# Three 256-column matmuls in place of a 512- and a 256-column one, and products summed to SBUF before the norm is applied

## The chip, the cores and the metric

One NeuronCore of a Trainium2 chip runs the program. The metric is the device time of one execution in microseconds (us); of several executions the median stands. The profile comes from one more execution. Engines: TensorE (PE, with its weight loads PEld), VectorE (DVE), ScalarE (ACT), GpSimd (POOL), and SyncE (SP), whose queue issues the weight transfers.

## What is computed

Two transformer blocks, one after the other, on 256 tokens of width 1024, in float32. The reference in short:

```python
x = x + 0.5 * swiglu(rms_norm(x, ffn1_norm), ...)             # first feed-forward, inner width 2816
z = rms_norm(x, mix_norm) @ w_in + b_in                       # first mixer: window attention and mLSTM
x = x + merged(z) @ w_out
x = rms_norm(x + 0.5 * swiglu(rms_norm(x, ffn2_norm), ...), final_norm)   # second feed-forward
h = x
proj = rms_norm_2(h, norm_mix_2) @ w_in_2                     # second mixer: gated linear attention and MLA
h = h + concat(o_gla, o_mla) @ w_out_2
h = h + cross_attention(rms_norm_2(h, norm_xa_2), mem) @ xa_w_o_2
g = conv3(rms_norm_2(h, norm_ffn_2) @ ffn_w_gate_2)           # third feed-forward, convolved along the tokens
h = h + (silu(g) * (rms_norm_2(h, norm_ffn_2) @ ffn_w_up_2)) @ ffn_w_down_2
```

## The kernel before

The activation `x` stays in SBUF, transposed: eight tiles of 128 features by 256 tokens, held in four pairs `x2[0..3]`. Every weight is read from HBM once, in chunks of up to 1 MB, by `wraw` (L327, three buffers `wr`). `halves` (L337) splits each chunk into a rounded part `wh`, by a ScalarE copy (L345), and the rest `wl`, by a VectorE subtraction (L346); both have six buffers. Activations are split in the same way by `split` (L458); a split tile holds the high part in `[:, 0]` and the low part in `[:, 1]`.

A product is the sum of high·high, high·low and low·high. `mm3` (L365) does this for one 128x128 block of a weight with two matmuls: `wh` against both parts side by side (512 columns: the left 256 get high·high, the right 256 high·low), then `wl` against the high part, added into the right 256. So one block of a product fills a PSUM bank of 512 columns in two parts, and `joined` (L520) adds them: ScalarE copies the right part to SBUF (L526), VectorE adds the left part (L527), and, if a norm `r` is given, VectorE multiplies it in (L529). `lin_t` (L377) is a product of 256 output features (2 x 8 blocks) into one PSUM tile of two banks; `lin_first` (L404) is the same with its last two blocks held back, into two tiles of another pool; `lin_n` (L386) computes with tokens in the partitions, three matmuls a block.

PSUM has eight banks. The pool `mm` has two tiles of two banks (`pm`, L228), the pool `at` four tiles of one bank (`pa`, L235). A tile is given again when all its readers have finished.

The norm factor `r` of a stage is ready late: squares, a sum on TensorE, `rsqrt` on GpSimd (L427, eleven small instructions) and `by_token` (L507), which spreads it over the partitions with TensorE. Products are therefore computed from the unnormalised `x`, and the norm is multiplied in when a product is joined.

The stages, in `program` (L1490): `ffn`, `mix` (L610), `ffn`, `mix2` (L966, with `mix2_heads` L998 and `xa` L1374), `ffn` with the convolution. In `ffn` (L533), `products(pr)` computes a gate and an up product and keeps both PSUM tiles in `pairs`; the loop at L565 joins, multiplies and splits them into `ahl`. Then four output tiles `dp`, each 2 x 22 blocks (L591 to L601), are joined, scaled and added to `x2[dp]`, and `x_done` (L448) splits the two new tiles of `x` for the next stage; in the last stage a DMA each writes them out (L607). In `mix`, three query products are started early (L619 to L621); `biased` (L624) joins a product into a tile `z` (two buffers) with the norm, and ScalarE adds the bias into the tiles `aq` (L631). In `mix2`, after the heads, the output projection (`wo2`, L982 to L995) adds two parts to each `x[d]` (L993, L994); in `xa` four query products (L1385) take tiles of `at`, and the output projection (`xo`, L1464 to L1484) again adds two parts to each `x` (L1476, L1483).

The order of the instructions on each engine is not the order of the program text: a planner simulates the program at compile time and lists the instructions by readiness, with the program order as the priority. Each engine then runs its list strictly in order.

Of the kernel before, what the change touches and what calls it, by code (L numbers as in the profile page):

```python
# [15 lines left out]
ALU = mybir.AluOpType  # L16
# [171 lines left out]
class Builder:  # L188
# [4 lines left out]

    def __init__(self, ctx, tc, I, out):
# [8 lines left out]
        self.uid = 0  # L203
        self.fine = 1
# [23 lines left out]
    def pm(self):  # L228

        return self.mm.tile([P, 2, 512], F32, tag="mm", name=self.n("mm"))  # L230

    def banks(self):
        return [t[:, j, :] for t in (self.pm(), self.pm()) for j in range(2)]
# [143 lines left out]
    def lin_t(self, key, xs, kt=KD, early=False):  # L377

        hv = self.wcols(key, 2, kt, early=early)
        ps = self.pm()  # L380
# [5 lines left out]
    def lin_n(self, key, n, xs, kt=KD, pool=None):  # L386

        ps = [pool() for _ in range(TB)] if pool else self.pm()
        ps = ps if pool else [ps[:, b, :] for b in range(TB)]
# [143 lines left out]
    def ffn(self, f, half, nxt=None, conv=False, last=False, first=False, mem=False):  # L533
# [3 lines left out]
        with self.phase("ffn") as fp:  # L537
# [5 lines left out]
            def products(pr):  # L543
# [4 lines left out]
                pairs[pr] = pg, self.lin_t(f"{f}u{pr}", xs, early=first and pr == 0)  # L548
# [16 lines left out]
            for pr in range(KF // 2):  # L565
                if pr > 1:
                    products(pr)
                pg, pu = pairs.pop(pr)
                s = ft([P, 512], "s", 2)
                if conv:  # L570
                    g = ft([P, 2, T + 2], "g", 2)
                    nc.vector.memset(g[:, :, 0:2], 0.0)
                    self.joined(pg, g[:, :, 2:], r)
                    for j in range(2):
                        w = [self.col("cw3", 22 * t + 2 * pr + j) for t in range(3)]
                        sj = s[:, j * T:j * T + T]
                        nc.scalar.activation(sj, g[:, j, 2:], AF.Identity, scale=w[2], bias=self.col("cb3", 2 * pr + j))
                        nc.vector.scalar_tensor_tensor(sj, g[:, j, 1:T + 1], w[1], sj, ALU.mult, ALU.add)
                        nc.vector.scalar_tensor_tensor(sj, g[:, j, 0:T], w[0], sj, ALU.mult, ALU.add)
# [6 lines left out]
                self.split(ahl[:, :, 2 * pr:2 * pr + 2, :].rearrange("p s j t -> p s (j t)"), a)  # L586
# [4 lines left out]
            for dp in range(KD // 2):  # L591
                ps = self.pm()
# [942 lines left out]
```

## Time and profile before

| | us |
|---|---|
| three runs | 1047.07, 1042.86, 1040.52 |
| their median | 1042.86 |
| the profiled execution | 1041.34 |
| its span, first to last instruction | 1039.6 |
| PE busy in the span | 998.3 |
| DVE busy | 753.4 |
| ACT busy | 598.8 |

The profiled execution took 1.7 us more than its span, and 1.5 us less than the median of the runs. A busy PE counts each matmul from its start to its end; matmuls overlap, so the pace of the array is read from the starts. PEclk is the granted clock of TensorE as a share of 2.4 GHz; its mean over the span is 0.988.

### The profile page before, as it was taken

What the parts mean: (1) busy time and instruction counts of PE and PEld (TensorE: products, weight loads), DVE (VectorE), ACT (ScalarE), POOL (GpSimd) and SP (SyncE); (2) the same over time, 40 slices, a digit from 0 to 9 for tenths busy, and PEclk for the clock granted to TensorE, in tenths of its full rate; (3) what the DMA queues carried; (4) which work ended last, traced back from release to release, by engine and by line L of the source; (5) the groups of instructions that cost most, each with busy time, mean ns of one, the idle gap of its engine ahead of it and who ended that gap; (6) DMA issues with size and microseconds to landing.
All of it is one profiled execution on the core that took longest, in us unless ns stands there. A gap on an engine that the chain in (4) does not pass through costs nothing.

```text
span 1039.6 us, 14827 instructions
## 1 busy us (share of the span) xinstructions
PE 998.3 (96%) x5562; PEld 848.6 (82%) x5562; DVE 753.4 (72%) x1309; ACT 598.8 (58%) x1041; POOL 66.1 (6%) x200
## 2 busy tenths in 40 slices
PE   6999999989999999999999999999899889999997
PEld 5888888879776778878888888987677768888886
DVE  7877666657977558787777856779848677988752
ACT  5755544448756456645655644669735456666541
POOL 4200000010000001000100200022000301000000
PEclk9999999999999999999999999999999989999999
DMA  6754555544444324544555555456006325555450
GB/s 240 252 202 173 182 180 192 193 152 173 134 170 142 122 81 168 197 162 170 203 195 202 200 178 202 138 212 223 22 1 243 122 81 198 172 197 192 161 195 20
DMA packets 28504, 172.72 MB, mean 166 GB/s; under 512 B 3712, under 2 KB 5008, under 8 KB 10128
## 3 DMA queue, kind: packets, MB, share of 16 engines
q1 hardware_dynamic: 26640, 169.88, 45.9%
q10 hardware_dynamic: 1728, 1.88, 0.7%
q8 instruction: 43, 0.70, 0.3%
q14 instruction: 29, 0.24, 0.1%
q0 software_dynamic: 64, 0.02, 0.0%
HBM read 170.72 MB, written 1.05 MB: 165 GB/s over the span
## 4 chain that ended last, share of the span: by engine, by line
PE 88%; DVE 4%; DMA 2%; ACT 2%; POOL 1%; issue 1%; ACTq 0%; DVEq 0%
PE mm L368 44%; PE mm L369 22%; PE mm L373 3%; PE mm L375 3%; PE mm L374 3%; DVE wl L346 2%; PE at L368 2%; DMA wr<-in_wts 1%; PE at L666 1%; PE at L702 1%; PE at L369 1%; ACT wh L345 1%; PE at L697 1%; DMA x<-in_xt 1%; PE at L807 0%
## 5 line engine op out<-in xcount | busy, mean ns | idle before, releaser
L346 DVE TENSOR_TENSOR wl<-wr,wh 128x1024 fp32r<-128x1024 f32 (+5 forms) x380 | 393.2, 1046 | 192.2 <-ACT wh L345 190.5
L345 ACT ACTIVATE wh<-wr 128x1024 fp32r<-128x1024 f32 (+5 forms) x380 | 340.5, 915 | 317.8 <-PE mm L368 222.6
L368 PE MATMUL mm<-xs,wh 128*128 128x512 f32 x1296 | 459.5, 399 | 9.2 <-DVE z L527 4.6
L369 PE MATMUL mm<-xs,wl 128*128 128x256 f32 x1296 | 364.2, 281 | 0.2 <-DVE wl L346 0.2
L368 PEld LDWEIGHTS mm<-xs,wh 128*128 128x128 f32 x1296 | 244.6, 189 | 67.7 <-issue 10.8
L369 PEld LDWEIGHTS mm<-xs,wl 128*128 128x128 f32 x1296 | 246.2, 190 | 0.9 <-DVE wl L346 0.6
L368 PE MATMUL mm<-ahl,wh 128*128 128x512 f32 x528 | 184.3, 395 | 0.0
L369 PE MATMUL mm<-ahl,wl 128*128 128x256 f32 x528 | 147.7, 280 | 0.0
L368 PEld LDWEIGHTS mm<-ahl,wh 128*128 128x128 f32 x528 | 99.0, 188 | 23.0
L369 PEld LDWEIGHTS mm<-ahl,wl 128*128 128x128 f32 x528 | 99.7, 189 | 0.0
L373 PE MATMUL mm<-wh,xs 128*128 128x512 f32 (+2 forms) x160 | 60.9, 381 | 2.0 <-ACT wh L345 2.0
L375 PE MATMUL mm<-wh,xs 128*128 128x512 f32 (+2 forms) x160 | 60.9, 381 | 0.0
L374 PE MATMUL mm<-wl,xs 128*128 128x512 f32 (+2 forms) x160 | 60.8, 380 | 0.0
L368 PE MATMUL mm<-b,wh 128*128 128x512 f32 x128 | 45.7, 397 | 0.0
L373 PEld LDWEIGHTS mm<-wh,xs 128*128 128x128 f32 x160 | 30.1, 188 | 7.8 <-ACT wh L345 2.3
L369 PE MATMUL mm<-b,wl 128*128 128x256 f32 x128 | 36.1, 282 | 0.0
L368 PE MATMUL at<-xs,wh 128*128 128x512 f32 x64 | 27.0, 462 | 8.4 <-DVE xs L467 8.4
L375 PEld LDWEIGHTS mm<-wh,xs 128*128 128x128 f32 x160 | 30.1, 188 | 5.8 <-issue 1.0
L374 PEld LDWEIGHTS mm<-wl,xs 128*128 128x128 f32 x160 | 30.1, 188 | 4.9
L368 PEld LDWEIGHTS mm<-b,wh 128*128 128x128 f32 x128 | 24.0, 188 | 6.0 <-issue 0.8
L585 DVE TENSOR_TENSOR a<-s,a 128x512 f32<-128x512 f32 x33 | 22.7, 692 | 2.8 <-ACT s L582 1.4
L368 PE MATMUL mm<-vs,wh 128*128 128x512 f32 x64 | 22.6, 395 | 1.9 <-DVE z L527 1.5
(503 smaller groups left out, 1242.3 us busy)
## 6 DMA issues: line engine op xcount, KB each, us to landing
wr<-in_wts SPq DMA_DIRECT2D x141, 1024.0 KB, 4.8
wr<-in_wts SPq DMA_DIRECT2D x12, 768.0 KB, 4.1
wr<-in_wts SPq DMA_DIRECT2D x6, 512.0 KB, 4.1
wr<-in_memt SPq DMA_DIRECT2D x2, 1024.0 KB, 5.6
wr<-in_wts SPq DMA_DIRECT2D x2, 864.0 KB, 4.4
wr<-in_wts SPq DMA_DIRECT2D x6, 256.0 KB, 5.1
bb<-in_rows ACTq DMA_DIRECT2D x6, 256.0 KB, 3.4
wr<-in_wts SPq DMA_DIRECT2D x2, 544.0 KB, 3.5
```

Of the source, the lines that this page charges most:

```text
L345: nc.scalar.activation(hi[:, i:i + m], v[:, i:i + m], AF.Copy)
L346: nc.vector.tensor_tensor(lo[:, i:i + m], v[:, i:i + m], hi[:, i:i + m].bitcast(F32), ALU.subtract)
L368: mm(ps, wh, xs, start=start, stop=False)
L369: mm(ps[:, T:], wl, xs[:, 0, :], start=False, stop=stop)
L373: mm(ps, xh, wh, start=start, stop=False)
L374: mm(ps, xh, wl, start=False, stop=False)
L375: mm(ps, xl, wh, start=False, stop=stop)
L585: nc.vector.tensor_tensor(a, s, a, ALU.mult)
L666: nc.tensor.matmul(ps[:, i * nk:i * nk + nk], aq[p][g * per + i][hs, b * P:b * P + P], ak[p][hs, 0:nk], start=True, stop=True)
L697: nc.tensor.transpose(pt[:, j * P:j * P + P], S[:, j, kb * P:kb * P + P], self.ident)
L702: nc.tensor.matmul(po[hs, :], av[:, kb, kv * 64:kv * 64 + 64], pTs[kb], start=kb == 0, stop=kb == b)
```

## The change

Five edits:

- `mm3` has a second form, for an output of 256 columns: three matmuls of 256 columns (`wh`·high, `wh`·low, `wl`·high) into the same columns, so that PSUM holds the finished sum. It is used in the last output tile of each `ffn` (`dp == 3`), in the last tile of `w_out` in `mix` (`wo3`), and, in the second mixer, in `gk`, `gq`, all of `wo2`, the four queries and all of `xo`. That is 3 x 44 + 16 + 32 + 64 + 32 + 32 = 308 blocks.
- Where the short form is used, the readers take one PSUM operand instead of two.
- `bank()` gives out a `pm` tile in two halves. The second mixer's PSUM users take halves instead of whole tiles, and the queries move from the pool `at` to `mm`.
- In `ffn`, gate and up products are joined to SBUF tiles (`s` or `g`, and `a`) right after each product, and `r` is multiplied into SBUF in the loop.
- In `mix`, the query and key products are joined straight into their `aq` and `ak` tiles; norm and bias are then applied in place.

```diff
+    def bank(self):
+
+        if self.half is None:
+            t = self.pm()
+            self.half = t[:, 1, :]
+            return t[:, 0, :]
+        h, self.half = self.half, None
+        return h
...
     def mm3(self, ps, wh, wl, xs, start, stop):
 
         mm = self.nc.tensor.matmul
-        mm(ps, wh, xs, start=start, stop=False)
-        mm(ps[:, T:], wl, xs[:, 0, :], start=False, stop=stop)
+        if ps.shape[-1] == T:
+            mm(ps, wh, xs[:, 0, :], start=start, stop=False)
+            mm(ps, wh, xs[:, 1, :], start=False, stop=False)
+            mm(ps, wl, xs[:, 0, :], start=False, stop=stop)
+        else:
+            mm(ps, wh, xs, start=start, stop=False)
+            mm(ps[:, T:], wl, xs[:, 0, :], start=False, stop=stop)
...
-        ps = self.pm()
+        ps = self.bank().rearrange("p (j t) -> p j t", j=2) if one else self.pm()
...
-                pairs[pr] = pg, self.lin_t(f"{f}u{pr}", xs, early=first and pr == 0)
+                if conv:
+                    s = ft([P, 2, T + 2], "g", 2)
+                    nc.vector.memset(s[:, :, 0:2], 0.0)
+                    self.joined(pg, s[:, :, 2:])
+                else:
+                    s = ft([P, 2, T], "s", 2)
+                    self.joined(pg, s)
+                a = ft([P, 2, T], "a", 2)
+                self.joined(self.lin_t(f"{f}u{pr}", xs, early=first and pr == 0), a)
+                pairs[pr] = s, a
...
-                    self.joined(pg, J(s), r)
+                    nc.vector.tensor_tensor(s, s, self.bc2(r), ALU.mult)
                 nc.scalar.activation(s, s, AF.Silu)
-                a = ft([P, 512], "a", 2)
-                self.joined(pu, J(a))
                 nc.vector.tensor_tensor(a, s, a, ALU.mult)
...
-                ps = self.pm()
+                short = dp == KD // 2 - 1
+                ps = self.pm()[:, :, :T if short else 2 * T]
...
-                y = self.joined(ps, J(ft([P, 512], "dy", 2)), rh)
-                nc.vector.tensor_tensor(J(self.x2[dp]), J(self.x2[dp]), y, ALU.add)
+                y = ft([P, 2, T], "dy", 2)
+                if not short:
+                    self.joined(ps, y, rh)
+                    nc.vector.tensor_tensor(J(self.x2[dp]), J(self.x2[dp]), y, ALU.add)
                 for j in range(2):
                     d = dp * 2 + j
+                    if short:
+                        nc.vector.tensor_tensor(y[:, j, :], ps[:, j, :], rh, ALU.mult)
+                        nc.vector.tensor_tensor(x[d], x[d], y[:, j, :], ALU.add)
...
+            def product(key, name, ps=None):
+
+                return self.joined(ps or self.lin_t(key, xs), mt([P, 2, T], name))
+
+            def biased(t, bias):
+
+                nc.vector.tensor_tensor(t, t, self.bc2(rB), ALU.mult)
+                for j in range(2):
+                    nc.scalar.activation(t[:, j, :], t[:, j, :], AF.Identity, bias=self.col("bin", bias + j))
+                return [t[:, j, :] for j in range(2)]
...
-                ps = self.lin_t(f"wo{dp}", [gs[:, :, k, :] for k in range(8)])
+                short = dp == 3
+                ps = self.lin_t(f"wo{dp}", [gs[:, :, k, :] for k in range(8)], one=short)
...
-                    ps = self.banks() if c == 0 else [self.pa() for _ in range(4)]
+                    ps = [(self.bank, self.pa)[c]()[:, :T] for _ in range(4)]
...
-                        V.scalar_tensor_tensor(x[d], x[d], gf[:, d:d + 1], ps[j][:, :T], ALU.mult, ALU.add)
-                        V.tensor_tensor(x[d], x[d], ps[j][:, T:], ALU.add)
+                        V.scalar_tensor_tensor(x[d], x[d], gf[:, d:d + 1], ps[j], ALU.mult, ALU.add)
...
-        pgk = self.lin_t("gk", xs)
+        pgk = self.lin_t("gk", xs, one=True)
...
-        self.joined(pgk, J(gk), rB)
-        self.joined(pgq, J(qd), rB)
+        V.tensor_tensor(J(gk), pgk, self.bc2(rB), ALU.mult)
+        V.tensor_tensor(J(qd), pgq, self.bc2(rB), ALU.mult)
...
-            pq = self.pa()
+            pq = self.bank()[:, :T]
...
-            nc.scalar.activation(u, pq[:, T:], AF.Copy)
-            V.tensor_tensor(u, pq[:, :T], u, ALU.add)
+            nc.scalar.activation(u, pq, AF.Copy)
...
-            for i in range(2):
-                V.tensor_tensor(x[j], ps[j][:, i * T:i * T + T], x[j], ALU.add)
+            V.tensor_tensor(x[j], ps[j], x[j], ALU.add)
             self.x_done(j)
```

Left out of the diff: `gq`, `wo3`'s reader and the second half of `xo`, which change like their neighbours; `xa_turn`, the state chain, the score tiles and `po` of `mix2_heads`, which take `bank()` where they took `pm()`; the convolution loop, rewritten without a change of what it issues but for the multiplication by `r`; and the gate tiles `g1` of `mix`, merged in pairs, so that four instructions of 512 columns stand for eight of 256.

## Rows read from the trace of the kernel before

**Rows 1.** The page, parts 1 and 4: busy time; the chain that ended last.

```profile
PE 998.3 (96%) x5562; PEld 848.6 (82%) x5562; DVE 753.4 (72%) x1309; ACT 598.8 (58%) x1041; POOL 66.1 (6%) x200
...
PE 88%; DVE 4%; DMA 2%; ACT 2%; POOL 1%; issue 1%; ACTq 0%; DVEq 0%
```

**Rows 2.** Waits, TensorE alone: who waited for whom, us in total, times, longest.

```profile
PE at L368 <- DVE xs L467: 8.4, 2, 7.3
PE mm L368 <- DVE z L527: 6.1, 2, 4.6
PE mm L368 <- DVE xs L467: 3.4, 1, 3.4
...
PE mm L373 <- ACT wh L345: 2.0, 1, 2.0
...
PE mm L368 <- DVE a L527: 1.3, 1, 1.3
```

**Rows 3.** Windows: length, then PE, PEld, DVE, ACT, POOL busy, PEclk, DMA share, GB/s.

```profile
224.00:230.00 6.00, 1.42 (x9) 1.17 (x9) 3.39 (x6) 3.60 (x8) 0.00 (x0) 0.99 0.54 203
230.00:234.00 4.00, 4.00 (x15) 3.37 (x15) 1.03 (x2) 1.83 (x5) 0.00 (x0) 0.59 0.00 0
...
836.00:841.00 5.00, 2.96 (x18) 2.35 (x16) 4.97 (x12) 5.00 (x11) 0.00 (x0) 0.99 0.00 0
841.00:851.00 10.00, 7.53 (x21) 5.81 (x22) 9.90 (x26) 4.83 (x10) 0.00 (x0) 0.50 0.58 210
776.00:788.00 12.00, 12.00 (x70) 10.44 (x69) 12.00 (x26) 8.57 (x17) 0.00 (x0) 1.00 0.51 163
```

**Rows 4.** Timeline, first mixer's beginning, all engines: start us, us, instruction, count [idle before].

```profile
216.56 1.22 DVE L346 TENSOR_TENSOR wl<-wr,wh 128x1024 fp32r<-128x1024 f32 x1
...
224.19 0.60 PE L512 MATMUL at<-ident,rN 128*128 128x128 f32 x4
...
225.60 1.29 DVE L529 TENSOR_TENSOR z<-z,rB 128x512 f32<-128x512 f32 x2
...
227.93 1.05 ACT L526 ACTIVATE z<-mm 128x512 f32<-128x512 f32 x2
...
229.38 0.47 PE L368 MATMUL mm<-xs,wh 128*128 128x512 f32 x1 [4.58 <-DVE z L527]
```

**Rows 5.** Timeline, TensorE alone, three places: how fast matmuls follow each other.

```profile
17.45 0.40 PE L369 MATMUL at<-xs,wl 128*128 128x256 f32 x2
17.68 0.40 PE L368 MATMUL at<-xs,wh 128*128 128x512 f32 x1
...
149.76 0.40 PE L368 MATMUL mm<-ahl,wh 128*128 128x512 f32 x1
...
156.84 0.40 PE L368 MATMUL mm<-ahl,wh 128*128 128x512 f32 x1
...
236.57 0.29 PE L373 MATMUL mm<-wh,xs 128*128 128x272 f32 x1
...
242.61 0.39 PE L368 MATMUL mm<-xs,wh 128*128 128x512 f32 x1
```

**Rows 6.** Groups by line, weight loads: count | busy us, mean ns | idle before.

```profile
L369 PEld LDWEIGHTS mm<-xs,wl 128*128 128x128 f32 x1296 | 246.2, 190 | 0.9 <-DVE wl L346 0.6
```

**Rows 7.** Groups by line and shape, VectorE: the adds of the last attention's output.

```profile
L1483 DVE TENSOR_TENSOR x<-at,x 128x256 f32<-128x256 f32 x8 | 3.3, 418 | 0.0
L1476 DVE TENSOR_TENSOR x<-mm,x 128x256 f32<-128x256 f32 x8 | 3.2, 419 | 3.0 <-PE mm L369 3.0
```

**Rows 8.** Timeline, the third feed-forward's beginning: start us, us, instruction [idle before].

```profile
841.72 0.48 DVE L467 SCALAR_TENSOR_TENSOR xs<-x,cols,xs 128x256 fp32r<-128x256 f32 x1
...
846.07 0.80 PE L368 MATMUL at<-xs,wh 128*128 128x512 f32 x1 [1.13 <-DVE xs L467]
```

**Rows 9.** Timeline, the end of the program.

```profile
1033.36 0.60 ACT L526 ACTIVATE dy<-mm 128x512 f32<-128x512 f32 x1 [14.04 <-PE mm L369]
...
1035.44 0.69 DVE L601 TENSOR_TENSOR x<-x,dy 128x512 f32<-128x512 f32 x1
```

More of the change, by code (lines that the diff above doesn't have):

```diff
@@ L203, in __init__ @@
         self.uid = 0
+        self.half = None
         self.fine = 1
@@ L228, in pm @@
     def pm(self):
+        self.half = None
         return self.mm.tile([P, 2, 512], F32, tag="mm", name=self.n("mm"))
-    def banks(self):
-        return [t[:, j, :] for t in (self.pm(), self.pm()) for j in range(2)]
+    def bank(self):
[5 more added lines that the diff above has]
+        return h
     def pa(self):
@@ L386, in lin_n @@
     def lin_n(self, key, n, xs, kt=KD, pool=None):
-        ps = [pool() for _ in range(TB)] if pool else self.pm()
-        ps = ps if pool else [ps[:, b, :] for b in range(TB)]
+        ps = [(pool or self.bank)() for _ in range(TB)]
         for k, kk, runs in n_runs(n, kt):
@@ L618, in mix @@
             acc = self.squares(self.x2)
-            early = {"aq00": self.lin_first("aq00", xs), "aq01": self.lin_t("aq01", xs)}
+            def product(key, name, ps=None):
[5 more added lines that the diff above has]
+                return [t[:, j, :] for j in range(2)]
+            aqs = {"aq00": product("aq00", "aq00", self.lin_first("aq00", xs)), "aq01": product("aq01", "aq01")}
             rN, _ = self.rinv_n(self.mean(acc, "ms"))
-            early["aq10"] = self.lin_t("aq10", xs)
+            aqs["aq10"] = product("aq10", "aq10")
             rB = self.by_token(rN)
-            def biased(key, bias, names):
-                ps = early[key] if key in early else self.lin_t(key, xs)
-                z = self.joined(ps, r=rB)
-                out = []
-                for j in range(2):
-                    t = mt([P, T], names[j])
-                    nc.scalar.activation(t, z[:, j, :], AF.Identity, bias=self.col("bin", bias + j))
-                    out.append(t)
-                return out
             aq = [[], []]
@@ L638, in mix @@
                 for jj in range(2):
-                    aq[p] += biased(f"aq{p}{jj}", 4 * p + 2 * jj, [f"aq{p}{2 * jj}", f"aq{p}{2 * jj + 1}"])
-            ak = biased("ak", 8, ["ak0", "ak1"])
+                    key = f"aq{p}{jj}"
+                    aq[p] += biased(aqs[key] if key in aqs else product(key, key), 4 * p + 2 * jj)
+            ak = biased(product("ak", "ak"), 8)
             av = mt([P, TB, 256], "av")
@@ L860, in mix @@
                 self.split(hs_[:, :, 2 * dp:2 * dp + 2, :].rearrange("p s j t -> p s (j t)"), ps)
-            g1 = [mt([P, T], f"aq{d // 4}{d % 4}") for d in range(KD)]
+            g1 = [mt([P, 2, T], f"aq{dp // 2}{dp % 2}") for dp in range(4)]
             for dp in range(4):
@@ L871, in mix @@
                 ym = self.joined(ps)
-                for j in range(2):
-                    nc.vector.scalar_tensor_tensor(ym[:, j, :], g1[2 * dp + j], 1.0, ym[:, j, :], ALU.add, ALU.mult)
+                nc.vector.scalar_tensor_tensor(ym, g1[dp], 1.0, ym, ALU.add, ALU.mult)
                 nc.vector.tensor_tensor(ym, ym, ya[:, 2 * dp:2 * dp + 2, :], ALU.add)
@@ L1213, in mix2_heads @@
         kk = self.xa_keys(ts, g2)
-        pt = self.pm()[:, 0, :]
+        pt = self.bank()
         for b in range(TB):
@@ L1221, in mix2_heads @@
         nc.scalar.activation(keN.rearrange("p b f -> p (b f)"), pt, AF.Copy)
-        pts = self.pm()
-        pts = [pts[:, r, :] for r in range(2)]
+        pts = [self.bank(), self.bank()]
         for c in range(2):
@@ L1280, in mix2_heads @@
         grs = mt([P, TB, 4], "grs")
-        po = self.pm()
-        po = [po[:, b, :] for b in range(TB)]
+        po = [self.bank(), self.bank()]
         for b in range(TB):
@@ L1464, in xa @@
         hv = self.wcols("xo0", 4, 4, per=2)
-        ps = self.banks()
+        ps = [self.bank()[:, :T] for _ in range(4)]
         out(ps, hv, [(0, j) for j in range(4)])
```

38 lines of the change are left out of this document (18 added, 20 removed).

## The prediction, written before the changed kernel was run

> **What bounds the kernel now.** I read the page first: PE is busy 96% of the span and holds 88% of the chain that ended last [rows 1]. So time falls only where PE works less or waits less. Next come the waits of PE alone [rows 2]: the reader sees a handful of places. Of the 8.4 us on the activation split, 7.3 us are the load of the first input, which nothing here touches. The others are 4.6 us on `z` (one wait of the 6.1), 3.4 us on `xs` at the third feed-forward, 2.0 us on weights and 1.3 us on `a`. Then the windows around these places [rows 3], to see what each wait does to the clock and which engine is full meanwhile, and last the timeline of each place [rows 4, 8, 9]. The sum is made against the profiled execution, 1041.3 us (span 1039.6), which is 1.5 us under the median of the runs.
>
> **Part 1, the pace of the short block.** A long block is one 512- and one 256-column matmul: from 149.76 to 156.84 us, 20 such blocks start [rows 5], 0.354 us each, and two 256-column matmuls take from 17.45 to 17.68 us, 0.115 each. Three of those make 0.345 us. The nearest run of short matmuls with a new weight load each is the 48 of 272 columns from 236.57 to 242.61 us [rows 5], 0.126 each; three make 0.378 us, and scaled by 256/272 0.355. Over 308 blocks the ends are 308 x (0.345 - 0.354) = -2.8 us and 308 x (0.378 - 0.354) = +7.4 us. The same number of columns streams in both forms, and the scaled value gives +0.3 us; I take 0.
>
> The third matmul brings a third weight load, and a load lasts 190 ns [rows 6]. Two loads of 190 ns don't fit one after the other with the matmuls into 0.354 us, so they run beside matmuls.
>
> The Trainium skill speaks against this (page "TensorE: Matmul & The Clock Gate", Part 3, on what overlaps): weight loads overlap running matmuls only when the row groups differ, and here every load takes all 128 rows. By its section on LDWEIGHTS, a load of 128 columns takes 128/1.2 = 107 ns, so by this rule an estimate is 308 x 0.107 = 33 us more. The 0.354 us of a block with two loads does not agree with the rule; it is kept as a rival below.
>
> **Part 2, the first mixer's beginning.** PE runs out of work at 224.8 us, right after the four matmuls of `by_token`, and starts again at 229.38 [rows 4]: 4.58 us. In between, VectorE multiplies `rB` into two `z` tiles, ScalarE then copies two PSUM tiles out, and only with them is an `mm` tile free. Both `z` buffers hold joined products that wait for the norm, so no PSUM tile can be emptied before it. The change gives each product its own `aq` tile and joins it without the norm: that dependence goes. The next product's weights were split by 217.8 us [rows 4], so PE has work at once; the next PSUM tile is needed one product (16 blocks, 5.7 us) later. After the stall the granted clock falls: from 230 to 234 us 15 matmuls start at a mean of 0.59 [rows 3], which at 0.177 us each (half a block) would take 2.7 us instead of 4.0. Together 4.6 + 1.3 = **5.9 us**; bounds 0 (the wait passes to another resource) and 6.
>
> **Part 3, the third feed-forward's beginning.** `xo` is added to `x` by 16 instructions of 0.42 us [rows 7], amid weight splits, while VectorE is busy 4.97 of 5 and 9.90 of 10 us [rows 3]. PE waits for the split behind these adds, 3.4 us [rows 2] ended by the one at 841.72, and 1.1 us more at 846.07 [rows 8]. Eight adds go. In the timeline 13 of the 16 start before the second wait ends; half of them, 6.5 x 0.42 = 2.7 us, is what PE gets back. From 841 to 851 the granted clock is 0.50, the lower level of 1.2 GHz, all along: 21 matmuls keep PE busy 7.5 us [rows 3] and would need 21 x 0.177 = 3.7; 3.8 us are lost to the clock. With a stall of 3.4 - 2.0 us (five adds fewer before the first) it may fall for a shorter time; I take half, 1.9. Together **4.6 us**; bounds 0 (other work fills VectorE) and 8 x 0.42 + 3.8 = 7.2.
>
> **Part 4, `wo2`.** Eight adds go here too, where VectorE is busy 12.00 of 12 us [rows 3]. The weights behind the 2.0 us wait [rows 2] are requested when VectorE frees a buffer; two of the eight adds stand before that, so **0.8 us**; bounds 0 and 2.0.
>
> **Part 5, the end.** After the last matmul come four instructions in a row, from 1033.36 to 1035.44 + 0.69 = 1036.13 us [rows 9]: 2.8 us. In the change the first half of the tile is finished earlier (its matmuls end 6 blocks before), and behind the last matmul stand one multiplication and one add of 256 columns, 2 x 0.42 us by rows 7. That gives **1.9 us**; bounds 1.4 and 2.2.
>
> **What I cost at nothing.** Earlier joins in `ffn`: the same instructions, under a PE without idle time in the loop; if that cover went, see the fourth rival. The last tiles of the first two `ffn` and `wo3`: PE does not wait at those borders, so their shorter ends buy nothing. `gk` and `gq`: two ScalarE copies and two VectorE adds fewer, but their PSUM tile is held until the norm; PE does not wait there today. Queries: one add less each, but PSUM from the two `mm` tiles instead of the four `at` tiles, which the key and value product `xv` and `xo` need too; I set gain against loss, 0, bounds -2 and +5 (somewhat more than the 3.4 us of the longest wait [rows 2]). Halves of PSUM tiles: more tiles free, but two users must finish before one is given again.
>
> **The sum.** 5.9 + 4.6 + 0.8 + 1.9 = 13.2 us. From 1041.3 that leaves 1028.1; with the 1.5 us that the median stands above, 1029.6, so 1030 us.
>
> **Rivals.**
>
> 1. *The planner leaves the copies in `mix` behind the multiplication by the norm.* The order of each engine's list is made from a simulation, so the joins could stay queued behind work that waits for `rB`. For: the two copies at 227.93 [rows 4] come after two multiplications. Against: the `z` buffers force that order now. Then 5.9 us are missing: 1036 us.
> 2. *The stalls move.* PE, released sooner, waits for weights instead, or the clock falls anyway. For: ScalarE is full from 836 to 841 us [rows 3]; 2.0 us of waiting are for weights [rows 2]. Against: in Part 2 the weights are there. Left are 2.7 + 1.9 us: 1042.9 - 4.6 = 1038 us.
> 3. *More than forecast.* All upper ends, with the 1.3 us wait on `a` gone and the faster pace: 6 + 7.2 + 2 + 2.2 + 1.3 + 2.8 = 21.5: 1021 us.
> 4. *Slower: the feed-forward loop waits for its SBUF tiles.* `g` or `s` and `a` have two buffers; a product's PSUM can only be emptied when the pair two before it is through. Place: pairs 2 to 10 of three `ffn`, 27 turns. Price: such a wait stands in the trace once, 1.3 us on `a` [rows 2]; 27 x 1.3 = 35 us, so 1030 + 35 = 1065 us. It decides from 13.2 / 27 = 0.49 us a turn. Against: `a` and `g` have two buffers today as well, and only one turn waits.
> 5. *Slower: the third weight load is not hidden.* 308 x 0.19 us [rows 6] = 58.5 us: 1088 us. Against: the 272-column matmuls with a load each, 0.126 us [rows 5], bound it at 7.4 us. This is the rule of the Trainium skill's page named above, at the trace's duration of a load.
>
> **How the numbers follow.** My forecast gets 0.52, the rivals in their order 0.12, 0.20, 0.08, 0.06 and 0.02. About 1% is what a measurement of this kernel can tell from no change: faster means under 1032.4 us. Most of the forecast's own width (1024 to 1036) lies below that, 0.44; with the third rival and small parts of the first two it makes 0.57. Rivals 4 and 5 give 0.07 for slower, a little being kept for milder forms; 0.36 remains. The range goes from 1022, near the third rival, to 1041, which holds the first two with a new stall of 3 us; it leaves out the slower rivals and the extremes, about 0.15.
>
> **What would show it.** Right: no PE wait on `z` near 225 us and no stretch of lower clock behind it; PE's waits on `xs` at the third feed-forward together under 2.5 us; about 1 us of instructions behind the last matmul; three 256-column matmuls of a block starting within 0.345 to 0.355 us of the next block's; PE matmuls 5562 + 308. Wrong: the wait near 225 us under another name; new PE waits between 690 and 840 us that together exceed 5 us; waits on `a`, `g` or `s` in the feed-forward loops; a short block above 0.37 us.

## The result, and the profile of the changed kernel

The changed kernel takes **1029.22 us** (median of 4 runs, 1026.66 to 1031.59) where the kernel before takes 1042.0 (4 runs, 1040.52 to 1047.07): a ratio of 0.9868, 95% interval 0.9822 to 0.9914. Measured a second time beside the last experiments (e9), where the kernel before took 1043.05, it took 1030.25 (6 runs, 1025.27 to 1036.24), a ratio of 0.9875, 0.9834 to 0.9916. The forecast was 1030.

The page of the changed kernel, parts 1 and 4, as in [rows 1]:

```profile
PE 999.7 (97%) x5870; PEld 864.3 (84%) x5870; DVE 744.3 (72%) x1286; ACT 595.3 (58%) x1036; POOL 67.2 (7%) x200
...
PE 86%; DVE 5%; ACT 2%; DMA 2%; POOL 2%; issue 2%; DVEq 0%; ACTq 0%
```

PE has 308 matmuls more and is busy 1.4 us longer, though the span is 9.7 us shorter: what went is waiting. VectorE has 23 instructions fewer. The waits of PE, as in [rows 2] (the lines have moved: a long block is now L382 and L383, a short one L378 to L380, a joined add L541):

```profile
PE at L382 <- ACT xs L480: 7.3, 1, 7.3
PE at L1173 <- DVE qT L1161: 3.5, 1, 3.5
PE at L382 <- DVE xs L481: 2.3, 1, 2.3
PE at L383 <- DVE wl L355: 2.1, 2, 1.5
PE mm L382 <- DVE z L541: 1.5, 1, 1.5
PE mm L378 <- DVE st L1292: 1.3, 1, 1.3
PE mm L382 <- DVE a L541: 1.2, 1, 1.2
PE at L1459 <- DVE xv L1396: 0.9, 1, 0.9
...
PE mm L378 <- ACT usq L1417: 0.8, 1, 0.8
...
PE mm L378 <- ACT xm L480: 0.7, 1, 0.7
...
PE mm L379 <- DVE xm L481: 0.5, 1, 0.5
```

Gone are the 4.6 us on `z` in the first mixer (the 1.5 us that are left are the second wait of that row), and of the 3.4 + 1.1 us on `xs` at the third feed-forward 2.3 are left. New are waits in the second mixer: 3.5 us on `qT`, 1.3 on `st`, 0.9 on `xv`, 0.8 on `usq` and 0.7 + 0.5 on `xm`, together 7.7 us. Gone there are, besides the 2.0 us on weights of [rows 2] and 1.3 us on `kT`, these two (waits of PE, kernel before):

```profile
PE at L1147 <- ACT g2k L1353: 3.0, 1, 3.0
PE at L1428 <- DVE S L1421: 2.3, 1, 2.3
```

Then the windows, columns as in [rows 3]:

```profile
224.00:230.00 6.00, 6.00 (x37) 5.30 (x36) 4.54 (x7) 5.62 (x12) 0.00 (x0) 1.00 0.37 120
230.00:234.00 4.00, 4.00 (x33) 3.96 (x32) 3.05 (x4) 3.14 (x5) 0.00 (x0) 1.00 0.49 147
830.00:835.00 5.00, 3.94 (x34) 3.73 (x32) 4.08 (x10) 4.19 (x9) 0.00 (x0) 1.00 0.00 0
835.00:845.00 10.00, 8.81 (x51) 7.73 (x52) 8.99 (x21) 5.48 (x12) 0.00 (x0) 1.00 0.58 185
...
725.00:737.00 12.00, 10.03 (x71) 8.96 (x72) 10.59 (x38) 8.32 (x32) 2.36 (x11) 0.72 0.15 45
```

From 224 to 230 us PE is busy all 6.00 us (before: 1.42), and the granted clock stays at 1.00 behind it (before: 0.59). The third feed-forward begins 6 us earlier, at 836 us, and the ten microseconds there run at 1.00 where they ran at 0.50, the lower level of 1.2 GHz. The price is in the last row: behind the new wait on `qT` the mean is 0.72.

So that one place isn't blamed for another's gain, I cut every profile at the same six kinds of border, from the start times in its timeline, and this table carries the rest of the text. A: from the last matmul of the first feed-forward to the norm (`by_token`) of the second, so all of the first mixer. E: from the last matmul of the second feed-forward to the norm of the second mixer. B: from there to the last `xo` matmul. C: from there to the norm of the third feed-forward. D: from the last matmul to the end of the span. F: the three streams of a feed-forward from its norm to its last matmul, together. The start takes 36.5 to 38.8 us in all. Spans are given to 0.1 us, so D is good to 0.05.

```
us, profiled run           A       E       B       C      D     F       span
before                  297.23  29.62  149.24  31.68  6.55  488.77   1039.6
changed                 290.52  28.67  149.12  25.59  4.93  494.41   1029.9
changed, second time    290.56  28.71  147.41  27.12  4.91  492.70   1028.5
e1_mix_alone            291.16  29.63  149.64  31.70  6.62  493.21   1040.8
e2_mix_undone           297.08  28.67  145.26  25.48  4.93  491.96   1030.0
e3_mixer2_long          290.56  29.37  151.36  31.87  4.89  491.94   1037.2
e4_xo_long              290.57  28.67  146.64  31.89  4.89  491.97   1031.1
e5_queries_at           290.56  28.67  145.71  25.58  4.88  491.60   1024.2
e6_wo2_long             290.57  28.67  149.35  25.59  4.94  494.41   1030.5
e7_breaks               290.78  28.67  147.59  27.21  4.94  498.71   1035.2
e8_all_tails_short      290.57  28.67  148.80  27.08  4.86  496.00   1033.0
e10_tails_long          291.23  29.11  148.90  27.02  6.63  489.90   1030.1
e11_ffn_undone          290.57  28.67  148.94  27.14  4.91  490.88   1027.7
e12_best                291.34  29.13  144.77  27.08  4.24  491.85   1025.2
```

Between the first two rows A, E, B, C and D give 6.71 + 0.95 + 0.12 + 6.09 + 1.62 = 15.5 us. F takes 5.64 back and the start 0.15: 9.7 us.

B's 0.12 us is the difference of two larger numbers. Cut once more, at the second `by_token` of the second mixer (764.88 us before, 763.09 in the changed kernel), its first part, mainly the heads, grew from 75.44 to 78.56 us (second time 77.09), and its second part, with `wo2`, the queries and `xo`, shrank from 73.80 to 70.56 (70.32). In the changed kernel's second profile PE is busy 69.72 us in the first part where it was 68.06, at the same mean clock of 0.98, so that growth is busy time, not waiting; the first profile adds 1.5 us, at a mean clock of 0.93.

### The profile page after: what moved, and what is told of

The parts are those of the page before. It is cut to its first block, busy times and chain, and to the rows that moved or that the text cites. A ratio compares the mean times of both kernels' runs of the same rounds, so it can differ in the third digit from the quotient of the medians.

```text
span 1029.9 us, 15400 instructions
## 1 busy us (share of the span) xinstructions
PE 999.7 (97%) x5870; PEld 864.3 (84%) x5870; DVE 744.3 (72%) x1286; ACT 595.3 (58%) x1036; POOL 67.2 (7%) x200
## 4 chain that ended last, share of the span: by engine, by line
PE 86%; DVE 5%; ACT 2%; DMA 2%; POOL 2%; issue 2%; DVEq 0%; ACTq 0%
PE mm L382 39%; PE mm L383 20%; PE mm L378 3%; PE mm L379 3%; PE mm L380 3%; PE mm L387 3%; PE mm L389 3%; PE mm L388 3%; DVE wl L355 2%; DMA wr<-in_wts 1%; PE at L691 1%; PE at L727 1%; PE at L382 1%; ACT wh L354 1%; PE at L722 1%
## 5 line engine op out<-in xcount | busy, mean ns | idle before, releaser
L382 PE MATMUL mm<-xs,wh 128*128 128x512 f32 x1264 | 448.0, 399 | 1.2 <-DVE a L541 1.2
L383 PE MATMUL mm<-xs,wl 128*128 128x256 f32 x1264 | 355.4, 281 | 0.2 <-DVE wl L355 0.2
L382 PEld LDWEIGHTS mm<-xs,wh 128*128 128x128 f32 x1264 | 237.5, 188 | 59.1 <-issue 2.3
L383 PEld LDWEIGHTS mm<-xs,wl 128*128 128x128 f32 x1264 | 239.0, 189 | 0.9 <-DVE wl L355 0.6
L382 PE MATMUL mm<-ahl,wh 128*128 128x512 f32 x396 | 139.2, 397 | 0.0
L383 PE MATMUL mm<-ahl,wl 128*128 128x256 f32 x396 | 110.9, 280 | 0.0
L382 PEld LDWEIGHTS mm<-ahl,wh 128*128 128x128 f32 x396 | 74.4, 188 | 18.0
L383 PEld LDWEIGHTS mm<-ahl,wl 128*128 128x128 f32 x396 | 74.7, 189 | 0.0
L382 PE MATMUL mm<-b,wh 128*128 128x512 f32 x128 | 45.7, 397 | 0.0
L378 PE MATMUL mm<-ahl,wh 128*128 128x256 f32 x132 | 37.4, 283 | 0.0
L379 PE MATMUL mm<-ahl,wh 128*128 128x256 f32 x132 | 37.4, 283 | 0.0
L380 PE MATMUL mm<-ahl,wl 128*128 128x256 f32 x132 | 37.4, 283 | 0.0
L383 PE MATMUL mm<-b,wl 128*128 128x256 f32 x128 | 36.1, 282 | 0.0
L382 PE MATMUL at<-xs,wh 128*128 128x512 f32 x64 | 24.9, 427 | 9.6 <-ACT xs L480 7.3
```

The source lines that it names most:

```text
L378: mm(ps, wh, xs[:, 0, :], start=start, stop=False)
L379: mm(ps, wh, xs[:, 1, :], start=False, stop=False)
L380: mm(ps, wl, xs[:, 0, :], start=False, stop=stop)
```

## The experiments

Each edit is against the changed kernel, the first one excepted. The times are medians; the ratio is to the kernel before on the same chip, where it took 1046.14 us beside e1 to e4, 1045.00 beside e5 to e8 and 1043.05 beside e9 to e12. Across these three groups compare ratios, not times.

```
kernel                  us (lowest to highest)       ratio to before [95%]
e1_mix_alone            1038.69 (1034.93 - 1042.49)  0.9930 [0.9900, 0.9961]
e2_mix_undone           1030.71 (1029.58 - 1031.71)  0.9846 [0.9823, 0.9869]
e3_mixer2_long          1039.93 (1038.94 - 1040.22)  0.9936 [0.9917, 0.9955]
e4_xo_long              1034.94 (1032.93 - 1038.42)  0.9894 [0.9865, 0.9922]
e5_queries_at           1028.24 (1025.94 - 1030.19)  0.9853 [0.9817, 0.9888]
e6_wo2_long             1033.58 (1031.94 - 1036.24)  0.9907 [0.9870, 0.9944]
e7_breaks               1035.08 (1031.53 - 1036.91)  0.9910 [0.9882, 0.9938]
e8_all_tails_short      1032.76 (1031.67 - 1034.77)  0.9899 [0.9865, 0.9933]
e9_after_again          1030.25 (1025.27 - 1036.24)  0.9875 [0.9834, 0.9916]
e10_tails_long          1033.32 (1031.62 - 1034.70)  0.9899 [0.9866, 0.9932]
e11_ffn_undone          1029.40 (1024.62 - 1032.09)  0.9860 [0.9827, 0.9893]
e12_best                1027.43 (1023.29 - 1029.82)  0.9844 [0.9809, 0.9880]
```

**The first mixer: one part alone, and everything but that part.** e1 is the kernel before with the products' own tiles and early joins in `mix`, and with the gate tiles `g1`, which reuse these tiles, merged in pairs; e2 is the changed kernel without them.

```diff
-                z = self.joined(ps, r=rB)
...
+                return self.joined(ps or self.lin_t(key, xs), mt([P, 2, T], name))
...
+                nc.vector.tensor_tensor(t, t, self.bc2(rB), ALU.mult)
```

> The kernel before with one part of the change alone: in the first mixer the query and key products are joined without the norm into their own tiles. Theory (the two z buffers, which wait for the norm, held PSUM): the 4.6 us wait of TensorE on z near 225 us and the stretch at half clock behind it are gone, the first score matmul comes 6 us earlier than at 246.2, the time is 1042.0 - 6.3 = 1036 us. Rival (the stall moves to the next resource): the wait stands under another name, under 2 us are gained, 1040 us or more.

> The changed kernel with that part undone (query and key products joined with the norm through the two z tiles, gate tiles of 256 columns). Theory: a wait of TensorE on z of about 4.6 us is back near 225 us, with half clock behind it, and the first score matmul comes 6 us later than at 239.9; 1029.2 + 6.3 = 1035.5 us. Rival (the other parts of the change gave it, the earlier joins everywhere): within 2 us of 1029.

In A, where the edit is, both agree: the early joins alone shorten it from 297.23 to 291.16 us, 6.1; without them it is 297.08. In e2 the stall is back under its old name (waits of PE, and the windows around it, columns as above):

```profile
PE mm L382 <- DVE z L541: 5.0, 2, 3.5
```

```profile
223.00:229.00 6.00, 2.48 (x15) 2.05 (x14) 3.31 (x7) 3.60 (x8) 0.00 (x0) 0.84 0.47 156
229.00:235.00 6.00, 6.00 (x23) 5.09 (x23) 1.28 (x4) 2.77 (x5) 0.00 (x0) 0.60 0.29 119
```

PE idles 3.5 us and then runs at a mean clock of 0.60, as in [rows 3]. The total of e1 agrees as well, some 7 us under the kernel before beside it. That of e2 doesn't: it was expected at 1035.5 us and came to 1030.71, and its ratio to the kernel before, 0.9846, is no higher than the changed kernel's 0.9868 and 0.9875. So over the whole program the loss of 6.5 us in A can't be seen: B is 2 to 4 us shorter and F 0.7 to 2.5, in places that the edit doesn't touch. In F that is the pace of a stream, which is shown below. In B it is probably the planner, which can write another order once one part differs. From here on I read the stretch first and the total second.

**The second mixer: all of it, then its parts.** e3 puts `mix2` back to the long form and the old PSUM tiles, e4 only `xo`, e6 only `wo2`, e5 only the queries' PSUM pool.

```diff
 e4 -    V.tensor_tensor(x[j], ps[j], x[j], ALU.add)
    +    for i in range(2):
    +        V.tensor_tensor(x[j], ps[j][:, i * T:i * T + T], x[j], ALU.add)
 e6 -    V.scalar_tensor_tensor(x[d], x[d], gf[:, d:d + 1], ps[j], ALU.mult, ALU.add)
    +    V.scalar_tensor_tensor(x[d], x[d], gf[:, d:d + 1], ps[j][:, :T], ALU.mult, ALU.add)
    +    V.tensor_tensor(x[d], x[d], ps[j][:, T:], ALU.add)
 e5 -    pq = self.bank()[:, :T]
    +    pq = self.pa()[:, :T]
```

> The changed kernel with the whole second mixer as before: long blocks, two adds a tile, whole PSUM tiles, queries in the pool at. Theory (16 + 8 adds fewer on a full VectorE gave the gain there): from the norm of the second feed-forward to the norm of the third the changed kernel gained 4.9 us though its feed-forward ran 2.3 us slower in between, so 7 us are lost again: 1036 us; the wait of 3.5 us on qT near 727 us goes, the one of 3.4 us on xs before the third feed-forward and some 10 us at half clock come back. Rival (halves of PSUM tiles and the queries' new pool cost as much as the adds save): within 2 us of 1029.

> The changed kernel with long blocks and two adds a tile in the last attention's output alone (8 adds of 0.42 us come back). Theory: these adds set the start of the third feed-forward: its first matmul and the norm come 2.5 to 3 us later, and the clock may fall there again, up to 3.8 us more: 1032 to 1036 us. Rival (the start came earlier because queries, values and scores before it end earlier): the first matmul within 1 us of where the changed kernel has it, relative to the last matmul of the output, and at most 1 us on the time.

> The changed kernel with the four short query products back in the pool at. From the norm r of the second mixer (the by_token near 763 us) to the last matmul of the attention's output the kernel before took 73.8 us, the changed one 70.6 and the one with a long xo 69.6. Theory (the queries gain by the missing add and by leaving at to scores, turns and values, against what I had set to nothing): 1 to 2.5 us of those 3 to 4 are lost, 72 to 73 us in that stretch. Rival (the gain there comes from the eight adds of wo2 alone): the stretch stays at 69.5 to 71 us.

> The changed kernel with long blocks and two adds a tile in wo2 alone (8 adds come back on a VectorE that was full from 776 to 788 us). Theory, as forecast: 0.8 us are lost in the stretch from r's by_token to the last matmul of the attention's output, 70.4 to 71.5 us. Rival (these adds carry most of the 3 to 4 us gained there): 73 us or more.

e4 is the clearest run of the study: A, E and D are the changed kernel's, B and F are if anything shorter, and C is 31.89 us, that of the kernel before (31.68). Eight adds of 0.42 us on VectorE are worth 4.8 to 6.3 us there (the long blocks that e4 also brings back end where C begins). Its wait and its windows show how (e4):

```profile
PE mm L382 <- DVE xs L481: 3.4, 1, 3.4
```

```profile
834.00:839.00 5.00, 3.18 (x7) 2.05 (x8) 5.00 (x15) 1.65 (x4) 0.00 (x0) 0.50 0.69 218
839.00:850.00 11.00, 11.00 (x51) 9.48 (x50) 7.20 (x17) 5.53 (x13) 0.00 (x0) 0.76 0.25 92
```

VectorE is full, PE waits, and the clock is at 0.50 for all of the first window and about half of the second (11 x (1 - 0.76) / 0.5 = 5.3 us). In the changed kernel no part of this place runs below 1.00; in its second profile one short stretch does (windows of e9):

```profile
830.00:834.00 4.00, 1.74 (x11) 1.44 (x10) 4.00 (x13) 4.00 (x11) 0.00 (x0) 0.87 0.15 20
834.00:838.00 4.00, 4.00 (x19) 3.43 (x18) 4.00 (x9) 2.92 (x7) 0.00 (x0) 0.71 0.62 242
```

That is 4 x 0.13 / 0.5 + 4 x 0.29 / 0.5 = 3.4 us at the lower level, and C is 27.12 instead of 25.59 us: the same program, 1.5 us apart by the clock, with a wait of 2.3 us on `xs` ahead of it in both.

e6 and e5 are read in the second part of B, the stretch that their expectations name. In the six profiles of kernels whose edits leave the second mixer alone (the changed one twice, e7, e8, e10, e11) it takes 70.12 to 71.25 us. e6 has 72.30, between its theory and its rival, so the eight `wo2` adds cost 1.1 to 2.2 us. A wait for the split of `xm`, the input of the queries, stands behind them (waits of PE, e6; 0.7 us in the changed kernel):

```profile
PE mm L378 <- ACT xm L480: 2.2, 1, 2.2
```

The 2.0 us wait on weights, by which the prediction costed these adds, is gone in the changed kernel, and neither e6 nor e3 brings it back, so it did not hang on them.

e5 has 68.68 us, the shortest of all profiles and below what theory and rival of its expectation named: in the pool `at` the queries are faster. The changed kernel's waits on `usq`, where the next query waits until ScalarE has read a query tile, and on `xv` are gone; in their place stand shorter ones (waits of PE, e5):

```profile
PE at L1451 <- DVE S L1444: 0.5, 1, 0.5
PE at L1433 <- DVE os L478: 0.4, 1, 0.4
```

e12 below has the queries there too, lacks the same two waits and is second shortest, 69.19; the shortest with the queries in `mm` is e4, 69.59. So the move to `mm` cost 0.9 to 2.6 us, the planner's order included.

e3 took 1039.93 us where 1036 was expected. Against the changed kernel's two profiles it loses 6.3 or 4.8 us in C, 2.2 or 4.0 in B and 0.7 in E. It was expected to end the new 3.5 us wait on `qT`, and it doesn't (waits of PE, e3):

```profile
PE at L1178 <- DVE qT L1166: 3.5, 1, 3.5
```

So this wait doesn't come from the short forms of the second mixer. It isn't in e1, but stands in every alteration of the changed kernel except e12, so none of the parts undone singly brings it; what does stays open.

**The pace of a stream.** Between the two profiles of the changed kernel F differs by 1.7 us, among the altered kernels by up to 8.8 (4.5 without e7 and e8, whose edits lie in F). e7 adds a 1-column matmul ahead of each pair of products in the feed-forwards, to break the stream; e8 takes the short form in all output tiles of the feed-forwards; e9 is the changed kernel unaltered.

```diff
 e7 +    nc.tensor.matmul(self.pa()[:, 0:1], self.ones, self.one1, start=True, stop=True)
 e8 -    short = dp == KD // 2 - 1
    +    short = True
```

> The changed kernel with one more matmul of a single column (its result is not used) ahead of every gate product of the three feed-forwards, 33 in all. In the traces so far a stream of long blocks runs at 0.3467 or at 0.3533 us a block, one of the two for up to 370 blocks, and changes only where something else stands between the blocks. Theory (the pace is drawn anew at each break): the gate and up loops now show stretches of 32 blocks at either pace, changing at the added matmuls, no stretch of 250 blocks at one pace. Rival (the pace follows what VectorE, ScalarE and the transfers do in that loop): the whole loop of a feed-forward stays at one pace, or it changes without regard to the added matmuls. The time within 3 us of the changed kernel's either way.

> The changed kernel with short blocks in all four output tiles of each feed-forward: 396 more short blocks, and nine times a copy of 0.58 us on ScalarE and nine adds on VectorE less. Theory (a short block costs 6 ns more than a long one at the same pace: 0.353 against 0.347, 0.360 against 0.353): 396 x 0.006 = 2.4 us more, the ratio to before some 0.002 higher, nothing given back since TensorE does not wait there. Rival (the third weight load is not hidden when short blocks follow each other for long): 0.378 us a block or more, 8 to 75 us more. Other rival (the epilogues saved are worth more than the blocks cost): faster.

> The changed kernel itself, unaltered, so that the kernels of this call have it beside them. My theory: the time of single runs spreads over about 5 us (1026.7 to 1031.6 so far) because each long run of 512- and 256-column pairs keeps one of two paces, 0.3467 or 0.3533 us a pair, and takes one of them anew at each break; so the median is 1027 to 1031 us and the paces of the stages in this profile need not be those of the first profile. Rival: the pace belongs to the program; then the profile shows again 0.3533 in the first feed-forward, 0.3533 in most of the second, and the third beginning at 0.3467 and changing to 0.3533.

The same program, the same stretch of the first feed-forward, in two executions. First the changed kernel (timeline of PE, a start, then the instruction):

```profile
37.56 0.39 PE L382 MATMUL mm<-xs,wh 128*128 128x512 f32 x1
...
184.90 0.40 PE L382 MATMUL mm<-ahl,wh 128*128 128x512 f32 x1
```

417 blocks in 147.34 us: 0.3533 us each. Then its second time (e9):

```profile
37.98 0.40 PE L382 MATMUL mm<-xs,wh 128*128 128x512 f32 x1
...
182.89 0.40 PE L382 MATMUL mm<-ahl,wh 128*128 128x512 f32 x1
```

418 blocks in 144.91 us: 0.3467 us each. The granted clock is 1.00 in both. So the pace doesn't belong to the program, and one of two values holds for hundreds of blocks. In the feed-forwards of these two kernels there is a break wherever it changes. In e7 the planner gathered the added matmuls into bunches, and at one of them the pace changes (timeline of PE, e7):

```profile
508.08 0.40 PE L382 MATMUL mm<-xs,wh 128*128 128x512 f32 x1
...
518.14 0.39 PE L382 MATMUL mm<-xs,wh 128*128 128x512 f32 x1
...
518.83 0.72 PE L558 MATMUL at<-ones 128*128 128x1 f32 x6
...
519.85 0.40 PE L382 MATMUL mm<-xs,wh 128*128 128x512 f32 x1
...
586.63 0.40 PE L382 MATMUL mm<-xs,wh 128*128 128x512 f32 x1
```

29 blocks of 0.3469 us before it, 189 of 0.3533 behind it. But the sign that e7's theory named, no stretch of 250 blocks at one pace, did not come: with the added matmuls in bunches, 356 blocks in the first feed-forward and 372 in the third keep 0.353. So e7 doesn't show that every break draws the pace anew. Each added matmul also stands twice in the trace (5936 matmuls, 66 more), and the time is 4 to 6 us above the changed kernel's two medians where at most 3 were expected. Nor is a break needed. In the first mixer of e7 the pace changes with nothing between, where the blocks of one input tile, `xs`, are followed by those of another, `b` (timeline of PE, e7):

```profile
415.61 0.40 PE L382 MATMUL mm<-xs,wh 128*128 128x512 f32 x1
...
424.80 0.40 PE L382 MATMUL mm<-b,wh 128*128 128x512 f32 x1
...
440.42 0.39 PE L382 MATMUL mm<-b,wh 128*128 128x512 f32 x1
```

26 blocks of 0.3535 us, then 45 of 0.3470. The short block is indifferent to this in the output tiles (e8, the third feed-forward's):

```profile
964.90 0.28 PE L378 MATMUL mm<-ahl,wh 128*128 128x256 f32 x1
...
1027.90 0.28 PE L378 MATMUL mm<-ahl,wh 128*128 128x256 f32 x1
```

175 blocks in 63.00 us: 0.360 each. Its 396 additional short blocks cost 396 x (0.360 - 0.3533) = 2.7 us against the slower pace, and e8 is 2.5 to 3.5 us above the changed kernel's two medians, with intervals that overlap.

**What was costed at nothing, and a better version.** e10 takes the long form again in the last output tiles of the feed-forwards, e11 puts the feed-forwards' joins back behind the norm, and e12 makes four alterations at once: the queries in their old pool, the short tile only at the very end and with its two halves in two PSUM tiles, and two multiplications of the second mixer on GpSimd.

```diff
 e10 -    short = dp == KD // 2 - 1
     +    short = False
 e11 -    pairs[pr] = s, a
     +    pairs[pr] = pg, self.lin_t(f"{f}u{pr}", xs, early=first and pr == 0)
 e12 -    ps = self.pm()[:, :, :T if short else 2 * T]
     +    ps = [self.pa()[:, :T] for _ in range(2)] if short else [pt[:, 0, :], pt[:, 1, :]]
     -    V.tensor_tensor(ki, gk, ei, ALU.mult)
     +    nc.gpsimd.tensor_tensor(ki, gk, ei, ALU.mult)
```

> The last output tile of each of the three feed-forwards goes back to the 512- and 256-column form. Theory: only the very end gains from the short form. From the last PE instruction to the end of the span it takes 6.5 us again instead of 4.9, and the tail of the first and second feed-forward is some 0.2 us shorter each; together 1 to 1.5 us above the changed kernel. Rival (the short ends of the first two feed-forwards help what follows): the stretch from the first feed-forward's last tile to the first scores, 38.56 us, grows by over 1 us, and the total by 3 us or more.

> The joins of the feed-forward loops go back behind the norm: the two products of a pair stay in PSUM until the pair's turn, as in the kernel before. Theory (costed at nothing): the time is that of the changed kernel within 2 us, the first pairs of a feed-forward excepted no wait of PE changes; the stretches around the three norms stay within 0.5 us. Rival (the early joins free PSUM tiles at the beginning of each feed-forward, where three products wait for the norm): PE waits for a PSUM tile near the norm of the second and third feed-forward come back, 1 to 3 us, and the time is 1031 to 1035 us.

> The changed kernel with four alterations: the queries of the cross-attention in their former PSUM pool, the short form of the feed-forward's last tile only at the very end and with its two halves in two PSUM tiles of their own, and two multiplications of the second mixer moved from VectorE to GpSimd. Theory: the queries give 1 to 2 us; the first half of the last tile no longer waits for the last matmul, so from the last PE instruction to the end of the span it is 4.2 us or less instead of 4.9; the two multiplications, 0.4 to 0.8 us each on VectorE, take up to 1 us from the wait of 3.5 us for the transposed queries, or nothing if GpSimd is slower than the path. Together 2 to 4 us: 1025 to 1028 us. Rival: each of these sits off the path and the time is that of the changed kernel, 1027 to 1031 us.

e10: D is 6.6 us again, 1.7 more than in the changed kernel beside it. The time is 3.1 us above that kernel's, where 1 to 1.5 were expected, with intervals that overlap. The stretch named in its rival, up to the first scores, did grow, from 38.56 to 40.43 us, but 5 blocks of the next product had moved ahead of the scores (79 long blocks of the `mm` tiles start in it where 74 did), 1.7 us of work and no loss. Over the whole of A the short end of the first feed-forward is worth 0.67 us, and in E that of the second 0.4, so the theory that only the very end gains is wrong. That is where the remainder of A comes from: 6.1 of the joins and 0.6 of this.

e11: A, E, C and D are those of the changed kernel to 0.04 us, the time is 1029.40. B is 1.5 us longer, its first part at a mean clock of 0.93 where the changed kernel beside it has 0.98, and F is 1.8 us shorter, with other paces. No gain or loss of the feed-forwards' early joins is seen.

The end, first in the changed kernel, answering [rows 9] (timeline; last matmul, then what follows it):

```profile
1024.97 0.28 PE L380 MATMUL mm<-ahl,wl 128*128 128x256 f32 x1
1025.28 0.76 DVE L626 TENSOR_TENSOR dy<-mm,rh 128x256 f32<-128x256 f32 x2 [12.06 <-PE mm L380]
1025.96 0.75 DVE L627 TENSOR_TENSOR x<-x,dy 128x256 f32<-128x256 f32 x2
```

Both multiplications and both adds stand behind the last matmul, also those of the first half, whose own matmuls were done earlier. In e12 each half has a PSUM tile to itself:

```profile
1019.12 0.42 DVE L627 TENSOR_TENSOR dy<-at,rh 128x256 f32<-128x256 f32 x1 [9.91 <-PE at L380]
1019.58 0.43 DVE L628 TENSOR_TENSOR x<-x,dy 128x256 f32<-128x256 f32 x1
...
1020.96 0.28 PE L380 MATMUL at<-ahl,wl 128*128 128x256 f32 x1
1021.28 0.42 DVE L627 TENSOR_TENSOR dy<-at,rh 128x256 f32<-128x256 f32 x1 [1.27 <-PE at L380]
1021.74 0.42 DVE L628 TENSOR_TENSOR x<-x,dy 128x256 f32<-128x256 f32 x1
```

Now the first half is done before the last matmul starts, and D is 4.24 us instead of 4.91. B is 144.77 us, the shortest of all, with no wait on `qT` but one of 3.9 us on a tile that GpSimd makes:

```profile
PE mm L1246 <- POOL g2k L1228: 3.9, 1, 3.9
```

e12's median is 2.8 us under that of the changed kernel beside it, the lowest of all; the two intervals overlap, so that it is faster is likely and not shown. By stretches it has 2.6 us less in B, of which the planner's order may be a part, 0.7 less in D, which is its own doing, and 1.2 more in A and E for the two long tails. The wait on `qT` went, as hoped of the multiplications on GpSimd, but a longer one took its place. With the short tails of the first two feed-forwards kept it should save those 1.2 us too; that was not tried.

## Why the prediction was right

**Part 1, the pace.** Mis-sized by little: forecast 0, measured about +1.9 us. The short block takes 0.360 us (42 of them from 1009.25 to 1024.37 us in the changed kernel, and those of e8), in two short places 0.352, against the 0.354 of [rows 5]: 308 x 0.006. What the step missed altogether is that the long block has two paces, and [rows 5] show only one of them. F cost 5.6 us in the first profile and 3.9 in the second; 132 of the short blocks lie in F, 0.9 us by 0.0067 each, and most of the rest is the pace drawn in each stream (the kernel before had 0.3467 in its second and third feed-forward, the changed one 0.3533 in most of both).

**Part 2, the first mixer.** Right in size and mechanism for the stretch A: forecast 5.9, e1 gives 6.1. The wait is gone and so is the low clock behind it. Over the whole program e2 doesn't show it.

**Part 3, the third feed-forward.** Right: forecast 4.6, measured 6.1 and 4.6 in the two profiles, and e4 shows that the eight adds are all of it. By terms: the waits shrank by 4.5 - 2.3 = 2.2 us (forecast 2.7), and the low clock went wholly or to a third, 3.9 or 2.4 us by what is left of C's gain (forecast half of 3.8). That the shorter wait spares the clock altogether was the case that I had halved.

**Part 4, `wo2`.** Too small, and by another way: forecast 0.8, e6 gives 1.1 to 2.2 us. The step that was wrong is that these adds hold back the weights of the 2.0 us wait: it is gone with or without them. What they hold back is the split of `xm`.

**Part 5, the end.** Forecast 1.9, measured 1.6. One step was wrong: "the first half of the tile is finished earlier". It waits for the last matmul, because both halves are one PSUM tile; e12 shows it by giving them two.

**Costed at nothing.** True of the feed-forwards' joins (e11). Not true of the last tiles of the first two feed-forwards: "their shorter ends buy nothing" missed 0.7 + 0.4 us, though PE doesn't wait at those borders in the view of waits. Nor perhaps of `gk` and `gq`: e3 has 0.7 us more in E, where they begin. Nor of the queries, whose new pool cost 0.9 to 2.6 us (e5), inside the bounds of -2 and +5. No term was given for the heads of the second mixer, the first part of B, which grew by 1.7 to 3.1 us; what lengthened it stays open but for the 1.5 us at the lower clock (e2 and e12, with other orders, have 75.58 there).

**The sum.** The stretches A to E gave 15.5 us in both profiles (second time: 6.67 + 0.91 + 1.83 + 4.56 + 1.64 = 15.6) where 13.2 were forecast, and F took back 5.6 or 3.9. Forecast and median agree to 1 us because these two errors have opposite signs, and a large part of the second is the pace, which no step foresaw: so close an agreement is luck.

**What would show it.** No wait on `z` near 225 us, no low clock behind it, 5870 matmuls, 2.3 us of waits on `xs` (under 2.5): as written. The short block is 0.360 us where 0.345 to 0.355 was named, and 1.4 us of instructions stand behind the last matmul (1025.28 to 1026.71) where 1 was. The waits that are new between 690 and 840 us make 7.7 us, over the 5 named as a sign against, so that sign came. It didn't decide, because 8.6 us went from the same place (3.0 + 2.3 + 2.0 + 1.3); but B is indeed the stretch that kept least of its gain.

**The rivals.** The planner did move the copies (1 falls with e1). Stalls did move in the second mixer, 7.7 us of new waits for 8.6 that went, with a lower clock behind the longest; but A and C kept their gains, so 2 falls as a whole. No wait on `g` or `s` appears, and the one on `a` is still one of 1.2 us (4 falls). The third load is hidden: 132 loads of 192 ns at each of three lines, in blocks of 0.360 us (groups by line, changed kernel):

```profile
L380 PEld LDWEIGHTS mm<-ahl,wl 128*128 128x128 f32 x132 | 25.3, 192 | 0.0
L379 PEld LDWEIGHTS mm<-ahl,wh 128*128 128x128 f32 x132 | 25.3, 192 | 0.0
L378 PEld LDWEIGHTS mm<-ahl,wh 128*128 128x128 f32 x132 | 25.3, 192 | 0.1
```

Three loads of 192 ns are 0.576 us, more than the block lasts, so in these records they run beside matmuls and beside each other (5 falls). The rule of the Trainium skill on which that rival stood (page "TensorE: Matmul & The Clock Gate", Part 3: loads overlap running matmuls only when their row groups differ) does not agree with these rows; here every load takes all 128 rows, and the measurement decides.

## What to carry to other kernels

Take VectorE instructions away where PE waits for VectorE with its list full: there eight adds of 0.42 us were worth 5 to 6 us, because less of the lower clock stood behind the shorter wait (behind 3.4 us some ten at 0.50, behind 2.3 us none or 3.4), while the earlier joins of the feed-forwards, where PE has work anyway, bought nothing. Empty a PSUM tile before the value that it waits for, if the algebra lets that value be multiplied in later, and give halves that are to be finished separately a tile each. When an order is planned by a program, compare stretches between fixed borders, not totals: an edit in one place here moved others by 2 to 4 us.

## What the runs showed of the hardware that I had not expected

A stream of 512- and 256-column pairs runs at 0.3467 or at 0.3533 us a pair at the same granted clock of 1.00. In the feed-forwards the value holds up to the next break in the stream (370 pairs in the third one of the changed kernel) and can be another behind it; in the first mixer it also changed without a break, with the input tile (e7). It can differ between two executions of one program. Over the 417 pairs counted above the difference is 2.8 us (417 x 0.0067); an estimate for all three feed-forwards is three times that, 8 us, of the size of the spread between runs of one kernel (1025.27 to 1036.24 for the changed one). What decides the pace was not found.

The lower clock too differs between two executions of one program. Behind the wait on `qT` the changed kernel's first profile has a mean of 0.72 over 12 us, as shown above; its second has 0.86 (windows of e9):

```profile
725.00:737.00 12.00, 10.50 (x84) 8.87 (x85) 10.53 (x39) 7.29 (x26) 2.37 (x11) 0.86 0.16 45
```

The wait of 3.5 us ahead of it is the same in both.
